# Plain FFN pairs 4 and 5: un-normalized h2 in 512 columns, weights split a chunk ahead, Strassen blocks made in between

## The chip, the cores and the metric

The kernel runs on one core of a Trainium2 chip. The metric is the device time of one execution in microseconds, as the median of several runs. Beside the runs there is one profiled execution with a trace of every instruction. Its engines are TensorE (PE; its weight loads are shown as PEld), VectorE (DVE), ScalarE (ACT), GpSimd (POOL) and the DMA queues, which are fed from SyncE (SP), ScalarE and GpSimd.

## The reference

One layer of an encoder over 512 tokens of 2048 features: a mixing part (attention over a neighbourhood and a convolution, gated, projected, normalized, added), then a feed-forward part. The change lies in the feed-forward part:

```python
u = rms_norm(h, ffn_pre_g[l])
gate, up = jnp.split(u @ w_gate_up[l], 2, axis=-1)
f = (jax.nn.silu(gate) * up) @ w_down[l]
h = h + rms_norm(f, ffn_post_g[l])
```

All is in float32. `gate` and `up` have 5632 columns each, which are 44 tiles of 128; `rms_norm` divides each token by the root of its mean square and multiplies each feature by a gain.

## The kernel before

**Layout and number format.** Features lie on the 128 partitions and the 512 tokens along the row. Each operand of a product is split into a high part, a cast to the matmul's own float32 form, and a low part, the rest. A product is then three matmuls: high weight by low activation, high by high, and low weight by high activation. ScalarE makes the high parts and VectorE the low ones (for weights `wchunk`, L137, in chunks of 128x1024; raw, high and low tiles come from pools of 5, 3 and 3). `merged` (L171) puts the high and low part of 256 tokens side by side into one tile of 512.

**The feed-forward part.** The 44 pairs of a gate tile and an up tile, counted here from 1, are made in four ways, one after the other:

- Pairs 1 and 2 (`interleaved`, L205, called at L938) read h2 times the gain, split but not yet normalized (`u`, high and low in 512 columns for each of 16 row blocks), while h2 itself is still being made.
- Pair 3 (`gemm`, L184, called at L941) reads the same `u`. In the first part of its loop, behind the first eight row blocks of the gate tile, stands the broadcast of 1/rms (`by_column`, L378) and its copy to SBUF as `r3` (L943). The pairs 1 to 3 are multiplied by `r3` when they leave PSUM (L948, L949), gated (L950, L951) and stored to DRAM from ScalarE's queue (L952). Their tiles come from a pool of two.
- Pairs 4 and 5 are the plain stage (L956 to L979). Its weights come in eight chunks of two row blocks by four tiles. For each row block, VectorE multiplies h2 by the gain and by `r3` (L964), in place; then `merged` makes two tiles of it, one for each half of the tokens; then `plain` (L178) issues three matmuls of 256 columns for each of four weight tiles and two halves. The chunk order is that of the row blocks, 0 to 15. From row block 8 on, block c and block c + 8 are joined for the Strassen part: four differences (`winograd_t`, L222) and four merges of them. At its end the gate goes through Silu straight out of PSUM (L996) and is multiplied by the up tile (L997), and `activated` (L983) stores it.
- Pairs 6 to 44 (`strassen`, L276) use a scheme with seven products of half size (Winograd's form) on the blocks `b11`, `b2`, `b_t12`, `b_t34` made in the plain stage. The first of them takes its first weight quarter from `begun` (L271).

**What sets the order.** Each engine runs its instructions in order. The order on an engine comes from the program's order and a scheduler that moves instructions by their inputs, so it is shown below as it was built. Tiles of 128x512 come from one pool of 66 slots; an instruction that writes a tile of a full pool waits until the last reader of the tile before is done.

The core of the plain stage before:

```python
for k in range(2):
    i = 2 * c + k
    nc.vector.scalar_tensor_tensor(out=f[i], in0=f[i], scalar=col(C_FPRE, i), in1=r3, op0=ALU.mult, op1=ALU.mult)
    ...
    for n in range(4):
        s = slice((k * 4 + n) * P, (k * 4 + n + 1) * P)
        for m, cols in enumerate((A, B)):
            plain(pf[n][:, cols], hi[:, s], lo[:, s], moving[m], i + m == 0, i == KT - 1)
```

Of the kernel before, what the change touches and what calls it, by code (L numbers as in the profile page):

```python
# [48 lines left out]
FT = DFF // P  # L49
# [21 lines left out]
C_PRE, C_POST, C_FPRE, C_FPOST, C_LNG, C_LNB, C_BDW, C_WDW = 0, 16, 32, 48, 64, 72, 80, 88  # L71
# [4 lines left out]
def hybrid_block(ctx: ExitStack, tc, xT, vecs, rpb, mask, w_c0, w_qk, w_v, w_gg, w_cg, w_ao, w_co, w_out, w_g0, w_gu, w_dn, outT):  # L76
    nc = tc.nc
# [6 lines left out]
    at = ctx.enter_context(tc.tile_pool(name="at", bufs=4, space=PSUM))  # L84
# [24 lines left out]
    def abank(name):  # L109
        return at.tile([P, NT], F32, tag="at", name=name)  # L110
# [60 lines left out]
    def merged(src, name):  # L171

        t = slot(name, F32R)
        nc.scalar.copy(t[:, A], src)  # L174
        nc.vector.tensor_tensor(out=t[:, B], in0=src, in1=t[:, A].bitcast(F32), op=ALU.subtract)
        return t

    def plain(o, hi, lo, t, first, last):  # L178

        nc.tensor.matmul(o, hi, t[:, B], start=first, stop=False, skip_group_check=True)  # L180
        nc.tensor.matmul(o, hi, t[:, A], start=False, stop=False, skip_group_check=True)  # L181
        nc.tensor.matmul(o, lo, t[:, A], start=False, stop=last, skip_group_check=True)  # L182

    def gemm(outs, acts, name, n=None, more=None, cols=slice(0, NT), between=(), pin=False, raw=None, load=nc.sync.dma_start):  # L184

        n = n or len(acts)
        between = iter(between)
        for c in range(0, n, 8):
            w = min(8, n - c)
            while len(acts) < c + w:  # L190
                acts.append(more(len(acts)))
            for i, (ps, src) in enumerate(outs):
                hi, lo = wchunk(src[:, c * P : (c + w) * P], f"{name}_{i}_{c}", raw=None if c or i else raw, load=load)
                for k in range(w):
                    s = slice(k * P, (k + 1) * P)
                    ah, al = (t[:, cols] for t in acts[c + k])
                    first, last = c + k == 0, c + k == n - 1
                    mmul = nc.tensor.matmul(ps, hi[:, s], al, start=first, stop=False)  # L198
# [3 lines left out]
                    nc.tensor.matmul(ps, lo[:, s], ah, start=False, stop=last)  # L202
                next(between, lambda: None)()

    def interleaved(ps, hi, lo, acts, c, cols=slice(0, NT)):  # L205
# [5 lines left out]
        for k, n, i in order:  # L211
# [10 lines left out]
    def winograd_t(u1, u2, t12, t34):  # L222

        nc.vector.tensor_tensor(out=t12[:, A], in0=u1[:, B], in1=u1[:, A], op=ALU.subtract)
        nc.vector.tensor_tensor(out=t12[:, B], in0=u2[:, B], in1=t12[:, A], op=ALU.subtract)
        nc.vector.tensor_tensor(out=t34[:, A], in0=u2[:, B], in1=u1[:, B], op=ALU.subtract)
        nc.vector.tensor_tensor(out=t34[:, B], in0=u2[:, A], in1=t12[:, B], op=ALU.subtract)
# [150 lines left out]
    def by_column(r, name, blocks=range(NB), pin=False):  # L378

        pb = abank(f"{name}_b")  # L380
        for t in blocks:
            mmul = nc.tensor.matmul(
                pb[:, t * P : (t + 1) * P], r[:, t : t + 1].broadcast_to([P, P]), ident, start=True, stop=True
            )
# [28 lines left out]
    def col(c, i):  # L413
        return vec[:, c + i : c + i + 1]
# [55 lines left out]
    u, acc = [], None  # L470
# [446 lines left out]
    for c in (*range(SPLIT), *range(HT)):  # L917
# [23 lines left out]
    gemm(  # L941
        [(pf[4 + n], w_gu[n * FT + 2]) for n in range(2)], u, "f0",
        between=(lambda: nc.scalar.copy(r3, by_column(r, "r3", pin=True)),),  # L943
    )
    for j in range(3):
        t = stp.tile([P, 2, NT], F32, tag="S", name=f"sg{j}")
        t, up = t[:, 0], t[:, 1]
        nc.vector.tensor_tensor(out=t, in0=pf[2 * j], in1=r3, op=ALU.mult)  # L948
        nc.vector.tensor_tensor(out=up, in0=pf[2 * j + 1], in1=r3, op=ALU.mult)  # L949
        nc.scalar.activation(t, t, AF.Silu)  # L950
        nc.gpsimd.tensor_tensor(out=t, in0=t, in1=up, op=ALU.mult)  # L951
        nc.scalar.dma_start(a_d[j], t)  # L952

    b11, b2, b_t12, b_t34 = [], [], [], []  # L956
    pf = [bank(f"f1_{n}") for n in range(4)]
    for c in range(HT):
        hi, lo = wchunk(w_g0[1, c], f"f1_{c}")
        if c == HT - 1:  # L960
            first = begun(w_gu[5], "f5")
        for k in range(2):
            i = 2 * c + k
            nc.vector.scalar_tensor_tensor(out=f[i], in0=f[i], scalar=col(C_FPRE, i), in1=r3, op0=ALU.mult, op1=ALU.mult)  # L964
            if i < HT:
                moving = [merged(f[i][:, cols], f"b1{i}_{n}") for n, cols in enumerate((A, B))]
                b11.append(moving[0])
            else:
                moving = [merged(f[i][:, cols], f"b2{i}_{n}") for n, cols in enumerate((A, B))]
                b2.append(moving)  # L970
            for n in range(4):
                s = slice((k * 4 + n) * P, (k * 4 + n + 1) * P)
                for m, cols in enumerate((A, B)):
                    plain(pf[n][:, cols], hi[:, s], lo[:, s], moving[m], i + m == 0, i == KT - 1)
            if i >= HT:
                t12, t34 = slot(f"t12_{i}"), slot(f"t34_{i}")
                winograd_t(f[i - HT], f[i], t12, t34)
                b_t12.append([merged(t12[:, cols], f"t12{i}_{n}") for n, cols in enumerate((A, B))])
                b_t34.append([merged(t34[:, cols], f"t34{i}_{n}") for n, cols in enumerate((A, B))])  # L979

    row = [const.tile([P, NT], F32, name=f"row{n}") for n in range(2)]

# [9 lines left out]
                nc.gpsimd.tensor_tensor(out=row[n], in0=row[n], in1=sq, op=ALU.add)  # L992

    for j in range(2):
        t = slot(f"sg{3 + j}")
        nc.scalar.activation(t, pf[2 * j], AF.Silu)  # L996
        nc.vector.tensor_tensor(out=t, in0=pf[2 * j + 1], in1=t, op=ALU.mult)  # L997
        activated(3 + j, t)


# [308 lines left out]
def _layout(x, mix_pre_g, mix_post_g, w_in, rpb, w_attn_o, w_dw, b_dw, conv_ln_g, conv_ln_b, w_conv_o, w_out,  # L1309
# [7 lines left out]
    def vec(g):  # L1317
# [13 lines left out]
    rp = rp.reshape(H, ROWS, 2, EC, ROWS, 4 * EC).transpose(0, 2, 1, 3, 4, 5)  # L1331
    wi = w_in[0]

    gu = w_gate_up[0].reshape(KT // 2, 2, P, 2, FT, P)[:, :, :, :, (0, 1, 3, 4)].reshape(KT // 2, 2, P, 2, 2, 2, P)
    gu = gu.transpose(4, 0, 2, 1, 5, 3, 6).reshape(2, KT // 2, P, 8 * P)

    cw = wi[:, 3 * CONV : 5 * CONV].reshape(KT // 2, 2, P, 2, CT, P)[:, :, :, :, :2]
    cw = cw.transpose(0, 2, 1, 4, 3, 5).reshape(KT // 2, P, 8 * P)
# [40 lines left out]
```

## Time and profile before

| what | us |
|---|---|
| median of 3 runs (2488.69 to 2489.56) | 2489.06 |
| the profiled execution | 2488.73 |
| its span, first to last instruction | 2487.0 |
| pair 3 and the broadcast, 1184.0 to 1207.9 | 23.9 |
| plain stage, 1207.9 to 1254.0 | 46.1 |
| first Strassen pair, 1254.0 to about 1273.9 | 19.9 |

Times within the span are in microseconds from its start. In a row of the timeline stand the start, the duration, the engine, the line, the operation, the tile written and the tiles read (buffer numbers left out, so that `f` is a bank of PSUM or a block of h2, `u` the split blocks, `b` and `t` the merged blocks and differences), the shape and a count. Matmuls overlap: what a matmul adds to the stream is the distance to the next start, not its own duration. The granted TensorE clock was 0.997 of full speed over the span. The engines' busy times in the three stretches:

```profile
1184.00:1207.90 23.90, 23.90 (x114) 20.02 (x114) 17.69 (x30) 10.45 (x20) 3.61 (x3) 1.00 0.37 116
1207.90:1254.00 46.10, 46.10 (x386) 46.07 (x384) 46.10 (x104) 26.64 (x62) 4.50 (x3) 1.00 0.44 130
1254.00:1274.00 20.00, 19.87 (x115) 17.35 (x114) 17.81 (x22) 11.06 (x16) 0.85 (x1) 1.00 0.71 193
```

The columns are the stretch and its length, then the busy time and count of PE, PEld, DVE, ACT and POOL, the granted clock, the share of the DMA engines and GB/s.

### The profile page before, as it was taken

To read this page: it belongs to the slowest core of one execution; us is meant where nothing else is said; L and a number is where in the kernel's file an instruction comes from. 1 tells how busy PE (TensorE), PEld (TensorE's weight loads), DVE (VectorE), ACT (ScalarE), POOL (GpSimd) and SP (SyncE) were. 2 spreads that over 40 slices of the span, in tenths; PEclk is the share of its full clock that TensorE was granted. 3 is DMA by queue.
4 is the path that set the end of the run, shared out by engine and by line. 5 is a ranking of instruction groups with operands and counts; after the bars stand their busy time and mean duration, and the time that the engine had idled before them with its cause. 6 is when DMAs were issued, how large, how long until landed. Compare 5 with 4: busy or idle time off the path is not lost. (4 is left out here: it accounts for less than half of the span.)

```text
span 2487.0 us, 36171 instructions
## 1 busy us (share of the span) xinstructions
PE 2464.5 (99%) x13495; PEld 2140.7 (86%) x13495; DVE 2073.1 (83%) x2745; ACT 1246.5 (50%) x1940; POOL 489.1 (20%) x583
## 2 busy tenths in 40 slices
PE   9999999999999999999999999999999999999997
PEld 7888888888888888888988888888888888888887
DVE  5999887497777668878898888889898889989887
ACT  5223333365555434556455555555555565456553
POOL 0110242220000000021111111122222203532352
PEclk9999999999999999999999999999999999999998
DMA  6246332486667544669466656666666778888986
GB/s 213 91 144 202 103 106 95 136 265 193 188 190 229 183 147 136 199 227 294 134 171 183 179 165 178 181 196 215 208 192 199 216 236 240 235 228 253 229 225 191
DMA packets 165249, 472.37 MB, mean 190 GB/s; under 512 B 18769, under 2 KB 30929, under 8 KB 165073
## 3 DMA queue, kind: packets, MB, share of 16 engines
q1 hardware_dynamic: 109728, 334.02, 40.3%
q0 software_dynamic: 32928, 97.54, 18.6%
q10 hardware_dynamic: 22416, 38.50, 4.1%
q8 instruction: 106, 1.74, 0.3%
q14 instruction: 71, 0.57, 0.1%
HBM read 396.06 MB, written 71.30 MB: 188 GB/s over the span
## 5 line engine op out<-in xcount | busy, mean ns | idle before, releaser
L458 DVE SCALAR_TENSOR_TENSOR cv<-z,vec,cv 128x497 f32<-128x497 f32 (+14 forms) x240 | 188.3, 786 | 4.8
L992 POOL TENSOR_TENSOR row<-row,asq 128x512 f32<-128x512 f32 x30 | 54.8, 1825 | 400.7 <-ACT asq L991 400.7
L1147 POOL TENSOR_TENSOR ys<-ys,row 128x512 f32<-128x512 f32 x32 | 57.7, 1804 | 119.7 <-DVE ys L355 99.9
L147 ACT CAST whi_qk<-raw_qk 128x1024 fp32r<-128x1024 f32 x32 | 33.7, 1054 | 79.2 <-PE qk L201 58.1
L152 DVE TENSOR_TENSOR wlo_qk<-raw_qk,whi_qk 128x1024 fp32r<-128x1024 f32 x32 | 40.4, 1262 | 37.9 <-ACT whi_qk L147 37.7
L1014 POOL TENSOR_TENSOR an<-an,row 128x512 f32<-128x512 f32 x32 | 52.1, 1630 | 74.2 <-DMA an<-a_d 49.0
L147 ACT CAST whi_y<-raw_y 128x1024 fp32r<-128x1024 f32 x31 | 32.6, 1052 | 63.0 <-PE py L201 55.2
L543 POOL TENSOR_TENSOR bm<-braw,msk 128x64 f32<-128x64 f32 x96 | 52.9, 588 | 15.5 <-DMA braw<-in_rpb 15.5
L777 DVE TENSOR_TENSOR gg<-py,gg 128x512 f32<-128x512 f32 x32 | 21.8, 687 | 39.6 <-PE py L202 33.2
L198 PE MATMUL py<-ycl,whi_y 128*128 128x512 f32 x128 | 49.8, 389 | 0.0
L201 PE MATMUL py<-ych,whi_y 128*128 128x512 f32 x128 | 49.8, 389 | 0.0
L202 PE MATMUL py<-ych,wlo_y 128*128 128x512 f32 x128 | 49.8, 389 | 0.0
L152 DVE TENSOR_TENSOR wlo_y<-raw_y,whi_y 128x1024 fp32r<-128x1024 f32 x31 | 37.8, 1224 | 14.0 <-ACT whi_y L147 8.4
L466 POOL TENSOR_TENSOR csum<-csum,cv 128x512 f32<-128x512 f32 x7 | 12.7, 1817 | 141.3 <-DVE cv L458 141.3
L181 PE MATMUL f<-b,whi_f 128*128 128x256 f32 x128 | 36.2, 283 | 0.0
L182 PE MATMUL f<-b,wlo_f 128*128 128x256 f32 x128 | 36.2, 283 | 0.0
L180 PE MATMUL f<-b,whi_f 128*128 128x256 f32 x128 | 36.2, 283 | 0.0
L147 ACT CAST whi_ca<-raw_ca 128x1024 fp32r<-128x1024 f32 x12 | 12.6, 1053 | 46.3 <-PE cb L201 18.1
L580 ACT ACTIVATE sc<-sc,st 128x256 f32<-128x256 f32 x32 | 16.1, 505 | 30.8 <-DVE st L579 30.8
L1148 POOL DMA_DIRECT2D y_d<-ys x32 | 29.4, 919 | 9.4 <-POOL ys L1147 7.8
L808 POOL DMA_DIRECT2D m_d<-m x8 | 4.4, 556 | 135.2 <-ACT m L174 95.0
L147 ACT CAST whi_v<-raw_v 128x1024 fp32r<-128x1024 f32 x16 | 16.8, 1051 | 24.2 <-PE pv L531 17.5
(3252 smaller groups left out, 8763.3 us busy)
## 6 DMA issues: line engine op xcount, KB each, us to landing
raw_qk<-in_w_qk SPq DMA_DIRECT2D x32, 512.0 KB, 3.4
raw_w<-in_w_dn SPq DMA_DIRECT2D x24, 512.0 KB, 5.6
a_d<-sg ACTq DMA_DIRECT2D x44, 256.0 KB, 4.1
raw_v<-in_w_v SPq DMA_DIRECT2D x16, 512.0 KB, 4.4
gg<-g_d SPq DMA_DIRECT2D x32, 256.0 KB, 4.0
raw_y<-in_w_co SPq DMA_DIRECT2D x16, 512.0 KB, 3.6
raw_f<-in_w_g SPq DMA_DIRECT2D x16, 512.0 KB, 3.6
an<-a_d POOLq DMA_DIRECT2D x32, 256.0 KB, 5.5
```

Of the source, the lines that this page charges most:

```text
L147: ins = cast(hi[:, s], raw[:, s])
L152: nc.vector.tensor_tensor(out=lo[:, s], in0=raw[:, s], in1=hi[:, s].bitcast(F32), op=ALU.subtract)
L180: nc.tensor.matmul(o, hi, t[:, B], start=first, stop=False, skip_group_check=True)
L181: nc.tensor.matmul(o, hi, t[:, A], start=False, stop=False, skip_group_check=True)
L198: mmul = nc.tensor.matmul(ps, hi[:, s], al, start=first, stop=False)
L201: nc.tensor.matmul(ps, hi[:, s], ah, start=False, stop=False)
L202: nc.tensor.matmul(ps, lo[:, s], ah, start=False, stop=last)
L458: nc.vector.scalar_tensor_tensor(out=a[:, to], in0=z[:, fr], scalar=col(C_WDW, i * CW + w), in1=a[:, to], op0=ALU.mult, op1=ALU.add)
L543: nc.gpsimd.tensor_tensor(out=bm[:, o + i - i0], in0=raw[:, :, min(max(i, 0), 3) * EC : (min(max(i, 0), 3) + 1) * EC], in1=msk[:, o + i - ...
L992: nc.gpsimd.tensor_tensor(out=row[n], in0=row[n], in1=sq, op=ALU.add)
L1014: ins = nc.gpsimd.dma_start(t, a_d[DN_P + k]), nc.gpsimd.tensor_tensor(out=t, in0=t, in1=row[k // KT], op=ALU.mult)
L1147: tc.keep_in_program_order(nc.gpsimd.tensor_tensor(out=t, in0=t, in1=row[n], op=ALU.mult))
```

## The change

The plain stage reads `u`, the split but un-normalized blocks that the pairs 1 to 3 read, in 512 columns, and multiplies by `r3` at the end. Its chunks hold row blocks c and c + 8, for which the weights are laid out anew on the host. In a chunk the matmuls with the high weights come first and those with the low weights behind them. The weights of chunk c + 1 are loaded and split in front of the matmuls of chunk c. The Strassen blocks of c and c + 8 are made by `prepare`, two of them within pair 3 and the others behind chunk c - 2, with the differences made in place; the second halves of the first eight blocks are not merged any more. The broadcast of 1/rms moves up in pair 3. The pairs 1 to 3 are stored from GpSimd's queue instead of ScalarE's.

```diff
-                hi, lo = wchunk(src[:, c * P : (c + w) * P], f"{name}_{i}_{c}", raw=None if c or i else raw, load=load)
                 for k in range(w):
+                    (at or {}).get((c, i, k), lambda: None)()
...
+    def prepare(c):
+
+        u1, u2 = f[c], f[c + HT]
+        for i, t in ((c, u1), (c + HT, u2)):
+            nc.vector.scalar_tensor_tensor(out=t, in0=t, scalar=col(C_FPRE, i), in1=r3, op0=ALU.mult, op1=ALU.mult)
+        b11.append(merged(u1[:, A], f"b11{c}"))
+        b2.append([merged(u2[:, cols], f"b2{c}_{n}") for n, cols in enumerate((A, B))])
+        for out, x, y in (
+            (u1[:, A], u1[:, B], u1[:, A]), (u1[:, B], u2[:, B], u1[:, B]), (u2[:, B], u2[:, B], u1[:, A]), (u2[:, A], u2[:, A], u2[:, B])
+        ):
+            nc.vector.tensor_tensor(out=out, in0=x, in1=y, op=ALU.subtract)
+        b_t12.append([merged(u1[:, A], f"t12{c}_0"), merged(u2[:, B], f"t12{c}_1")])
+        b_t34.append([merged(u1[:, B], f"t34{c}_0"), merged(u2[:, A], f"t34{c}_1")])
+
+    w = []
+
+    def next_weights():
+        w.append(wchunk(w_g0[1, len(w)], f"f1_{len(w)}"))
+
     gemm(
         [(pf[4 + n], w_gu[n * FT + 2]) for n in range(2)], u, "f0",
-        between=(lambda: nc.scalar.copy(r3, by_column(r, "r3", pin=True)),),
+        at={(0, 0, 3): lambda: nc.scalar.copy(r3, by_column(r, "r3", pin=True))},
+        between=(lambda: None, lambda: prepare(0), lambda: prepare(1), next_weights),
     )
...
-        nc.scalar.dma_start(a_d[j], t)
+        nc.gpsimd.dma_start(a_d[j], t)
...
     for c in range(HT):
-        hi, lo = wchunk(w_g0[1, c], f"f1_{c}")
-        if c == HT - 1:
+        if c + 1 < HT:
+            next_weights()
+        else:
             first = begun(w_gu[5], "f5")
-        for k in range(2):
...
+        hi, lo = w[c]
+        acts = list(enumerate((u[c], u[c + HT])))
+        for part in range(2):
+            for k, (ah, al) in acts:
+                for n, ps in enumerate(pf):
+                    s = slice((k * 4 + n) * P, (k * 4 + n + 1) * P)
+                    if part:
+                        nc.tensor.matmul(ps, lo[:, s], ah, start=False, stop=c + k == HT, skip_group_check=True)
+                    else:
+                        nc.tensor.matmul(ps, hi[:, s], al, start=c + k == 0, stop=False, skip_group_check=True)
+                        nc.tensor.matmul(ps, hi[:, s], ah, start=False, stop=False, skip_group_check=True)
+        if c + 2 < HT:
+            prepare(c + 2)
...
-        t = slot(f"sg{3 + j}")
-        nc.scalar.activation(t, pf[2 * j], AF.Silu)
-        nc.vector.tensor_tensor(out=t, in0=pf[2 * j + 1], in1=t, op=ALU.mult)
+        t, up = slot(f"sg{3 + j}"), slot(f"su{3 + j}")
+        nc.vector.tensor_tensor(out=t, in0=pf[2 * j], in1=r3, op=ALU.mult)
+        nc.vector.tensor_tensor(out=up, in0=pf[2 * j + 1], in1=r3, op=ALU.mult)
+        nc.scalar.activation(t, t, AF.Silu)
+        nc.vector.tensor_tensor(out=t, in0=t, in1=up, op=ALU.mult)
```

Three places as the engines now have them. Names are those of the program with their buffer numbers; what an instruction waits for stands in brackets, by the engine or DMA queue that gives the signal.

TensorE at the plain stage, before: `f1_0` to `f1_3` are the four banks, `b10_0` and `b10_1` the merged halves of row block 0.

```order
L180 MATMUL f1_2_10966<-b10_0_10975,whi_f1_0_10969 128x256
L181 MATMUL f1_2_10966<-b10_0_10975,whi_f1_0_10969 128x256
L182 MATMUL f1_2_10966<-b10_0_10975,wlo_f1_0_10970 128x256
L180 MATMUL f1_2_10966<-b10_1_10978,whi_f1_0_10969 128x256
L181 MATMUL f1_2_10966<-b10_1_10978,whi_f1_0_10969 128x256
L182 MATMUL f1_2_10966<-b10_1_10978,wlo_f1_0_10970 128x256
```

And in the change, where the high weights of chunk 0 end and its low ones follow (`u2_8l` and `u2_8h` are row block 8 of `u`):

```order
L980 MATMUL f1_2_11026<-u2_8l_10614,whi_f1_0_11001 128x512
L981 MATMUL f1_2_11026<-u2_8h_10613,whi_f1_0_11001 128x512
L980 MATMUL f1_3_11027<-u2_8l_10614,whi_f1_0_11001 128x512
L981 MATMUL f1_3_11027<-u2_8h_10613,whi_f1_0_11001 128x512
L978 MATMUL f1_0_11024<-u2_0h_10351,wlo_f1_0_11002 128x512
L978 MATMUL f1_1_11025<-u2_0h_10351,wlo_f1_0_11002 128x512
```

Six matmuls of 256 columns on one bank became three of 512, and the third of them moved behind the chunk's sixteen with high weights.

VectorE in the change, from the second pass of the first gated tile (`sg0`) to the third tile (`sg2`), whose buffer is that of `sg0`:

```order
L959 TENSOR_TENSOR sg0_11006<-f0_1_10348,r3_10806 128x512
L958 TENSOR_TENSOR sg1_11012<-f0_2_10349,r3_10806 128x512
L959 TENSOR_TENSOR sg1_11012<-f0_3_10350,r3_10806 128x512
L152 TENSOR_TENSOR wlo_f1_1_11030<-raw_f1_1_11028,whi_f1_1_11029 128x1024 [waits DMAHW5_49,PE_49,Activation_49]
L935 SCALAR_TENSOR_TENSOR f2_10008<-f2_10008,vec_75,r3_10806 128x512
L935 SCALAR_TENSOR_TENSOR f10_10040<-f10_10040,vec_75,r3_10806 128x512 [waits DMAHW4_49]
L958 TENSOR_TENSOR sg2_11018<-f0_4_10818,r3_10806 128x512 [waits DMASW6_49,Pool_49]
```

Before, the row of `sg2` (L948) waited for a store from ScalarE's queue and stood eighteen rows behind the second pass of `sg0`; it now waits for one from GpSimd's (DMASW) and stands six rows behind.

VectorE at the start of pair 6, before (`f5l` are low weights, `f5s` and `f6s` weight sums, `f_1` and `f_3` banks, `f5v` copies out of PSUM):

```order
L266 TENSOR_TENSOR f5l<-f5s_11771,f5h 128x1024 [waits Activation_49]
L355 TENSOR_TENSOR sg_11845<-f_3_11703,f5c_11799 128x256 [waits Activation_49]
L288 TENSOR_TENSOR f6s_11891<-f6s_11857,f6q 128x1024 [waits DMAHW5_49,DMASW7_49,DVE_49]
L329 TENSOR_TENSOR f_1_11679<-f_1_11679,f5v_11726 128x512 [waits PE_49]
L266 TENSOR_TENSOR f5l<-f5s_11724,f5h 128x1024 [waits Activation_49]
```

And in the change:

```order
L254 TENSOR_TENSOR f5l<-f5s_11545,f5h 128x1024 [waits Activation_49]
L317 TENSOR_TENSOR f_1_11453<-f_1_11453,f5v_11500 128x512 [waits PE_49]
L254 TENSOR_TENSOR f5l<-f5s_11498,f5h 128x1024 [waits DVE_49,Activation_49]
L343 TENSOR_TENSOR sg_11619<-f_3_11477,f5c_11573 128x256 [waits DVE_49]
L276 TENSOR_TENSOR f6s_11665<-f6s_11631,f6q 128x1024 [waits DMAHW2_49,DMASW2_49,DVE_49]
```

The sum into the bank (L329, now L317) stood behind the weight sum of pair 7 (L288, now L276) and now stands three rows ahead of it.

More of the change, by code (lines that the diff above doesn't have):

```diff
@@ L176, in merged, with gemm @@
         return t
[L178 to L184, printed above, removed]
+    def gemm(outs, acts, name, n=None, more=None, cols=slice(0, NT), between=(), pin=False, raw=None, load=nc.sync.dma_start, at=None):
         n = n or len(acts)
@@ L220, in interleaved @@
                 follow(nc.tensor, mmul)
[L222 to L227, printed above, removed]
     def winograd_in_place(u):
@@ L940, in hybrid_block @@
     pf += [abank(f"f0_{n}") for n in range(4, 6)]
+    b11, b2, b_t12, b_t34 = [], [], [], []
+    def prepare(c):
[13 more added lines that the diff above has]
+        w.append(wchunk(w_g0[1, len(w)], f"f1_{len(w)}"))
     gemm(
         [(pf[4 + n], w_gu[n * FT + 2]) for n in range(2)], u, "f0",
-        between=(lambda: nc.scalar.copy(r3, by_column(r, "r3", pin=True)),),
+        at={(0, 0, 3): lambda: nc.scalar.copy(r3, by_column(r, "r3", pin=True))},
+        between=(lambda: None, lambda: prepare(0), lambda: prepare(1), next_weights),
     )
@@ L951, in hybrid_block @@
         nc.gpsimd.tensor_tensor(out=t, in0=t, in1=up, op=ALU.mult)
-        nc.scalar.dma_start(a_d[j], t)
-    b11, b2, b_t12, b_t34 = [], [], [], []
+        nc.gpsimd.dma_start(a_d[j], t)
     pf = [bank(f"f1_{n}") for n in range(4)]
     for c in range(HT):
-        hi, lo = wchunk(w_g0[1, c], f"f1_{c}")
-        if c == HT - 1:
+        if c + 1 < HT:
+            next_weights()
+        else:
             first = begun(w_gu[5], "f5")
-        for k in range(2):
[L963 to L979, printed above, removed]
+        hi, lo = w[c]
[11 more added lines that the diff above has]
+            prepare(c + 2)
     row = [const.tile([P, NT], F32, name=f"row{n}") for n in range(2)]
@@ L1332, in _layout @@
     wi = w_in[0]
-    gu = w_gate_up[0].reshape(KT // 2, 2, P, 2, FT, P)[:, :, :, :, (0, 1, 3, 4)].reshape(KT // 2, 2, P, 2, 2, 2, P)
-    gu = gu.transpose(4, 0, 2, 1, 5, 3, 6).reshape(2, KT // 2, P, 8 * P)
+    gu = w_gate_up[0].reshape(KT, P, 2, FT, P)
+    gu = [
+        gu[:, :, :, n : n + 2].reshape(*by, P, 2, 2, P).transpose(*order, 2, 1 - order[0], 4, 3, 5).reshape(KT // 2, P, 8 * P)
+        for n, by, order in ((0, (KT // 2, 2), (0,)), (3, (2, KT // 2), (1,)))
+    ]
     cw = wi[:, 3 * CONV : 5 * CONV].reshape(KT // 2, 2, P, 2, CT, P)[:, :, :, :, :2]
@@ L1354, in _layout @@
         w_out=tiles(w_out[0]),
-        w_g0=c(gu),
+        w_g0=np.stack(gu),
         w_gu=tiles(w_gate_up[0]),
```

## Prediction, made before the changed kernel ran

> **What bounds the kernel now.** I read the busy shares first, then what TensorE waited for, then the stage that the change touches by windows, then its rows one by one.
>
> ```profile
> PE 2464.5 (99%) x13495; PEld 2140.7 (86%) x13495; DVE 2073.1 (83%) x2745; ACT 1246.5 (50%) x1940; POOL 489.1 (20%) x583
> PE warm L123 <- POOL ident masks.py:199: 1.5, 1, 1.5
> ...
> PE r_s L365 <- ACT ysq L1223: 0.2, 1, 0.2
> 1207.93:1253.99 46.06, 46.06 (x385) 46.06 (x384) 46.06 (x104) 26.63 (x62) 4.50 (x3) 1.00 0.44 130
> ```
>
> The first row is the page's: TensorE is busy for 99% of the span. The next two are the first and the last of the twelve rows of what its matmuls waited for; the twelve add up to 8.2 us in 2487. The last is the windows' row of the plain stage of pairs 4 and 5 (columns: PE, PEld, DVE, ACT and POOL busy, granted clock, DMA share, GB/s). TensorE and VectorE are both busy for all of it and the granted clock is 1.00. So time can go here only where TensorE's own stream gets shorter; and VectorE, with no gap of its own, is the engine to watch for a new wait.
>
> A full row of digits does not say at what rate matmuls follow each other. That is in the starts:
>
> ```profile
> 1197.05 0.39 PE L198 MATMUL f<-u_8l,whi_f 128*128 128x512 f32 x1
> ...
> 1207.70 0.39 PE L202 MATMUL f<-u_15h,wlo_f 128*128 128x512 f32 x1
> 1207.93 0.28 PE L180 MATMUL f<-b,whi_f 128*128 128x256 f32 x1
> 1208.04 0.28 PE L181 MATMUL f<-b,whi_f 128*128 128x256 f32 x1
> ...
> 1253.88 0.28 PE L182 MATMUL f<-b,wlo_f 128*128 128x256 f32 x1
> 1254.00 0.40 PE L304 MATMUL f<-b,f5h 128*128 128x512 f32 x1
> ```
>
> From 1197.05 to 1207.93 stand the last 48 matmuls of pair 3, each over 512 columns: 10.88 / 48 = 0.2267 us from start to start. From 1207.93 to 1254.00 stand the 384 matmuls of the plain stage, each over 256 columns: 46.07 / 384 = 0.1200 us. Two of 256 columns take 0.2400, one of 512 takes 0.2267. Twice the columns cost 0.1067 more, so about 0.0133 us of each matmul has nothing to do with its columns (0.1200 - 0.1067).
>
> **The change part by part. TensorE's stream.** The 384 matmuls of 256 columns become 192 of 512, over the same columns in all. At pair 3's spacing, same operand forms and same tiles of h2, they take 192 x 0.2267 = 43.52 us in place of 46.07: **2.55 us less**, all of it on the path, as TensorE waits for nothing in the stage.
>
> The Trainium skill speaks against the size of this: "TensorE: Matmul & The Clock Gate", section Back-to-back issue gap, gives an isolated gap of N / 2.4 + 2.5 ns at full clock, which is 109.2 ns for 256 columns and 215.8 for 512. By that estimate the saving would be 192 x (218.4 - 215.8) = 0.5 us. The rows above differ from it (120.0 and 226.7 ns), and they decide.
>
> **Row of 1/rms sooner.** The broadcast of 1/rms goes from behind the first eight row blocks of the pair 3 GEMM to in front of the fourth, that is 15 matmuls or 3.4 us up.
>
> ```profile
> 1185.52 1.03 POOL L375 TENSOR_TENSOR r_r<-r_v,mhalf 128x4 f32<-128x4 f32 x1 [8.93 <-DVE r_v L373]
> 1187.28 0.39 PE L198 MATMUL f<-u_3l,whi_f 128*128 128x512 f32 x1
> 1190.68 1.05 PE L382 MATMUL r_b<-ident,r_r 128*128 128x128 f32 x8
> 1191.77 0.59 ACT L943 COPY r<-r_b 128x512 f32<-128x512 f32 x1
> 1132.38 1.63 POOL L375 TENSOR_TENSOR r_r<-r_v,mhalf 128x2 f32<-128x2 f32 x1 [12.13 <-DVE r_v L373]
> ```
>
> The power on GpSimd ends at 1186.55; TensorE now gets to the broadcast at 1187.28, where the row of the fourth block starts. That leaves 0.7 us. The same step took 1.63 at 1132.38, and would then end at 1187.15, still before. So no wait; the bound on the other side is 0.5 us, if the notice takes longer than I allow. The broadcast costs TensorE the same at either place. The row in SBUF is there at 1191.77 + 0.59 - 3.4 = 1188.96, and VectorE may begin 3 us sooner.
>
> **VectorE's and ScalarE's work.** The old code split both halves of all 16 blocks (32 merges); the new one leaves out the second half of the first eight, which nothing else reads: 8 merges less on each engine. The differences and their merges stay. The end of the stage gets four VectorE passes more (both pairs must now be multiplied by 1/rms), 4 x 0.60.
>
> ```profile
> 1192.87 0.68 DVE L948 TENSOR_TENSOR sg<-f,r 128x512 f32<-128x512 f32 x1
> 1193.47 0.68 DVE L949 TENSOR_TENSOR sg<-f,r 128x512 f32<-128x512 f32 x1
> 1230.30 0.41 DVE L224 TENSOR_TENSOR t<-f 128x256 f32<-128x256 f32 x1
> 1230.64 0.41 DVE L226 TENSOR_TENSOR t<-f,f 128x256 f32<-128x256 f32 x1
> 1237.48 1.40 DVE L964 SCALAR_TENSOR_TENSOR f<-f,vec,r 128x512 f32<-128x512 f32 x2
> 1238.80 0.74 DVE L175 TENSOR_TENSOR b<-f,b 128x256 fp32r<-128x256 f32 x2
> 1246.30 1.21 DVE L266 TENSOR_TENSOR f5l<-f5q,f5h 128x1024 fp32r<-128x1024 f32 x1
> 1247.44 1.08 DVE L175 TENSOR_TENSOR t<-t,t 128x256 fp32r<-128x256 f32 x3
> ```
>
> Start to start: 0.60 for a pass over 512 columns of PSUM, 0.34 for 256 columns, 0.66 for a scaling pass (1.32 for two), 1.14 for a weight's low part. From 1188.96 VectorE then has 16 scalings, 56 merges, 32 differences, 9 low parts and 6 passes over PSUM: 10.6 + 19.0 + 10.9 + 10.3 + 3.6 = 54.4 us, done at 1243.4 if nothing holds it. TensorE leaves the stage at 1207.93 + 43.52 = 1251.45. So there are 8 us to spare where there was no gap. Slots could eat some: h2 stays held for the stage, and later blocks wait until TensorE has used up a chunk. The last block may start when the sixth of eight chunks is done, at 1240.6, and needs about 5 us. That still ends by 1247. Cost: **nothing**. The sooner blocks buy nothing either, since TensorE did not wait for them.
>
> **The store that goes to another queue.** The three stores of gated tiles go from ScalarE's queue to GpSimd's. Their tiles come from a pool of two, so the first write of the third tile stands behind the first store, on VectorE, and its Silu stands on ScalarE ahead of the cast of the third weight chunk.
>
> ```profile
> 1194.30 1.29 POOL L951 TENSOR_TENSOR sg<-sg 128x512 f32<-128x512 f32 x1 [7.75 <-ACT sg L950]
> 1210.31 2.73 POOL L951 TENSOR_TENSOR sg<-sg 128x512 f32<-128x512 f32 x1 [12.32 <-ACT whi_f L147]
> 1223.90 0.91 POOL L253 DMA_DIRECT2D f5s<-in_w_gu  x1 [10.86 <-DMA f5s<-in_w_gu]
> y_d<-yf POOLq DMA_DIRECT2D x16, 256.0 KB, 3.9
> y_d<-y_d POOLq DMA_DIRECT2D x8, 512.0 KB, 9.2
> ```
>
> VectorE has 30 instructions up to the second half of the first tile (4 scalings, 22 of 256 columns, 2 low parts, 2 passes: 2.6 + 7.5 + 2.3 + 1.2 = 13.6 us), so the tile is whole at 1202.6. The product takes 1.3 to 2.7 us, the store 3.9 (the nearest, a plain store of this size) to 9.2 (the slowest of GpSimd's queue shown): free at 1207.8 to 1214.5. VectorE gets there at 1202.6 + 3.7 = 1206.3, and stands still for 1.5 to 8.2 us. The third chunk's cast then follows by 0.60 + 0.6 (Silu) + 1.05, at 1210.1 to 1216.8; A chunk is 24 matmuls, 5.44 us, and TensorE wants the third at 1207.93 + 2 x 5.44 = 1218.8. Hidden by 2 to 9 us; I take the near end. If that cover goes, each us later is a us of the total.
>
> The Trainium skill has a rule against this move: "SBUF — State Buffer", section SBUF: two separate sides, warns that a DMA issued by GpSimd can starve, as its descriptors need a port that VectorE may hold. By it the store could cost much more than 9.2 us. The row at 1223.90 has GpSimd issue one in 0.91 us while VectorE was busy without a gap, which speaks against that here.
>
> **The next pair.** In pair 6, the first of the Strassen part, TensorE waited once:
>
> ```profile
> 1262.97 1.21 DVE L288 TENSOR_TENSOR f6s<-f6s,f6q 128x1024 f32<-128x1024 f32 x1
> 1264.10 0.69 DVE L329 TENSOR_TENSOR f<-f,f5v 128x512 f32<-128x512 f32 x1
> 1264.82 0.59 ACT L293 COPY f5v<-f 128x512 f32<-128x512 f32 x1 [1.88 <-DVE f L329]
> 1265.46 1.01 PEld L304 LDWEIGHTS f<-t,f5l 128*128 128x128 f32 x8 [0.33 <-ACT f5v L293]
> ```
>
> The sum at 1264.10 stood behind a weight sum for pair 7 that took 1.13; in the new order it stands ahead of that. Walked from 1251.0, when the first bank of the stage is complete: five passes (3.0), a low part, a pass, a low part, a weight sum, a pass, a low part (4 x 1.14 + 2 x 0.60) bring VectorE to 1259.8; the product that the sum needs ends about 1260.1; the sum and the copy are done by 1261.5. TensorE wants them at about 1265.13 - 2.55 = 1262.6. So the 0.33 us go as well. Bounds: 0.33 gained, or up to 1 us lost if one cast comes late, as the margin is 1.1 us. I take the gain. Behind it, from pair 8 on, the engines' orders are the old ones.
>
> **Sum.** -2.55 - 0.33 = -2.88 us. The profiled execution took 2488.73 (span 2487.0 and 1.7 around it), 0.33 under the median of the three runs, 2489.06. Its span would be 2484.1, and the median **2486.2**.
>
> **The rivals.** *Columns are all that costs.* If what a matmul takes beside its columns doesn't halve with their number, 192 matmuls of 512 columns come out 0.2400 apart, and only the 0.33 us of pair 6 go: **2488.7**. Against it stand the 48 matmuls of pair 3; for it, a little, that the same shape ran slower for a stretch:
>
> ```profile
> 1151.59 0.40 PE L215 MATMUL f<-u_4h,whi_f 128*128 128x512 f32 x1
> ...
> 1152.98 0.84 PE L215 MATMUL f<-u_4l,whi_f 128*128 128x512 f32 x3
> ```
>
> These are six in 1.39 us, 0.232 each, which would leave 1.6 of the 2.55 us. This rival is also what the rule of the Trainium skill above comes close to.
>
> *The gain is taken back in pair 6.* The four new passes and two Silus stand in front of its weight casts, and the one wait of 0.33 us there becomes one of 1 to 2.5 us: **2487.5** to 2489. For: the margin is 1.1 us. Against: the walk above, with the weight sum out of the way.
>
> *Slower.* The store on GpSimd's queue holds VectorE and, by the Silu, the third weight cast. It decides from a store of 9.2 + 2.0 = 11.2 us on; from 14.1 the kernel is slower than before, as 2.9 us of gain are used up, and at 20 us it stands at 2486.2 + 8.8 = **2495**. For: VectorE is dense there, and a GpSimd product took 2.73 instead of 1.29 in that place. Against: the issue row and landings of 3.9.
>
> *More than the sum.* VectorE's spare 8 us let later stages run without waits. The twelve rows total 8.2 us, most of them far away (warm-up, the last norm), so more than 5 us in all would need nearly all of them to go: **2483**.
>
> That the change does not do what it says I leave out: the order shows 192 matmuls of 512 columns.
>
> **How the numbers follow.** A measurement of this kernel can tell about 0.2% from no change, which is 5.0 us here; the forecast of 0.12% lies inside. Forecast 0.72, columns alone 0.06, pair 6 takes it back 0.10, slower rival 0.08 (over half of it past 0.2%), more than the sum 0.04. Faster by over 0.2%: 0.05; within: 0.90; slower: 0.05. The forecast's bounds are 0.5 for the broadcast, 1.3 for pair 6 and some 0.4 between runs: 2485.0 to 2488. With the two rivals that give the gain back, the range goes from 2484.8 to 2489.0, and leaves out the slower rival, the faster one and a little more.
>
> **What would show it.** In the new profile: 192 matmuls from the first chunk to pair 6 in 43.5 us, 0.2267 apart; no wait at the broadcast in front of the fourth block; the third gated tile's first pass some us late on VectorE with no gap on TensorE behind it; no wait before pair 6's third sum with its copy. Wrong would be a gap on TensorE at the third or fourth chunk (the store), a spacing over 0.23, or a longer gap in pair 6.

## The result, and the profile after

The changed kernel takes **2484.77 us** (median of 19 runs, 2484.23 to 2487.94) against 2488.80 of the kernel before in the same runs (19, 2487.86 to 2492.44): ratio 0.9986 [0.9979, 0.9992], 4.0 us less. That is inside the 0.2% that was called no change, though the interval leaves out 1. It was forecast at 2486.2; the median lies 1.4 us under that and rounds to the low end of the range, 2484.8. So the size of the gain is what has to be explained: 2.9 us were forecast, and 4.0 came.

Where it came from can't be read off the span alone. The profiled executions took 2485.70 (span 2483.9) and 2488.73 (span 2487.0), but from one execution to another the part ahead of the plain stage and the part behind pair 7 differ by 1 us or more, while the stage and the pairs behind it repeat to some 0.02 us. So the stretches are compared one by one.

Of the kernel after: the page's row of busy time, then the windows' rows of the plain stage and of pair 6, in the columns used above, then TensorE's rows at the two ends of the stage.

```profile
PE 2462.1 (99%) x13303; PEld 2131.3 (86%) x13303; DVE 2073.4 (83%) x2741; ACT 1245.3 (50%) x1932; POOL 492.9 (20%) x586
```

```profile
1208.08:1251.60 43.52, 43.52 (x194) 36.04 (x193) 42.49 (x89) 23.51 (x51) 6.81 (x4) 1.00 0.52 143
1251.60:1271.10 19.50, 19.50 (x113) 17.20 (x112) 18.29 (x23) 11.42 (x16) 0.84 (x1) 1.00 0.71 215
```

```profile
1207.85 0.39 PE L197 MATMUL f<-u_15h,wlo_f 128*128 128x512 f32 x1
1208.08 0.39 PE L980 MATMUL f<-u_0l,whi_f 128*128 128x512 f32 x1
...
1251.60 1.98 PE L292 MATMUL f<-b,f5h 128*128 128x512 f32 x8
```

The stage takes 43.52 us where it took 46.07, and pair 6 takes 19.50 where it took 19.91 (1254.00 to 1273.91). That is 2.55 + 0.41 = 2.96 us. From pair 7 to pair 44, TensorE's starts lie 2.81 us earlier throughout, to 0.01 us (0.15 of the 2.96 was lost ahead of the stage, in that one execution). What is left of the 4.0 us has to lie elsewhere, and it was found at the very end. Here are the last row of VectorE (timeline, with the answer's heading that gives the span) and the issues of the last stores (name, queue, count, size, median us from issue to landing), first of the kernel before, then of the kernel after.

```profile
core 0 of [0], span 2487.0 us
2480.57 1.29 DVE L1287 TENSOR_TENSOR yg<-yg,hb 128x512 f32<-128x512 f32 x2
```

```profile
out<-yg ACTq DMA_DIRECT2D x3, 256.0 KB, 4.9
out<-hb POOLq DMA_DIRECT2D x1, 512.0 KB, 7.1
```

```profile
core 0 of [0], span 2483.9 us
2478.53 1.29 DVE L1293 TENSOR_TENSOR yg<-yg,hb 128x512 f32<-128x512 f32 x2
```

```profile
out<-yg ACTq DMA_DIRECT2D x3, 256.0 KB, 4.2
out<-hb POOLq DMA_DIRECT2D x1, 512.0 KB, 6.2
```

The last VectorE result is there at 2481.86 before and at 2479.82 after; the span ends 5.14 us later before, and 4.08 us later after. The last stores, which no line of the diff touches, land about 1 us sooner. Nothing in the prediction speaks of this; the section on the store below shows what moved.

### The profile page after: what moved, and what is told of

It is laid out like the page before. It is cut to its first block, busy times and chain, and to the rows that moved or that the text cites. A ratio compares the mean times of both kernels' runs of the same rounds, so it can differ in the third digit from the quotient of the medians.

```text
span 2483.9 us, 35789 instructions
## 1 busy us (share of the span) xinstructions
PE 2462.1 (99%) x13303; PEld 2131.3 (86%) x13303; DVE 2073.4 (83%) x2741; ACT 1245.3 (50%) x1932; POOL 492.9 (20%) x586
## 5 line engine op out<-in xcount | busy, mean ns | idle before, releaser
L1083 DVE TENSOR_TENSOR sg<-sg,su 128x512 f32<-128x512 f32 x39 | 28.9, 740 | 0.0
L193 PEld LDWEIGHTS py<-ycl,whi_y 128*128 128x128 f32 x128 | 24.0, 188 | 5.0
L197 PEld LDWEIGHTS py<-ych,wlo_y 128*128 128x128 f32 x128 | 24.0, 188 | 5.0
```

The costliest lines, as they stand in the source:

```text
L1083: nc.vector.tensor_tensor(out=t, in0=t, in1=up, op=ALU.mult)
```

## Experiments

Each kernel's stretches, from the starts on TensorE and the last VectorE result ("end"), in us, and its median less that of the kernel before in the same runs. "Sum" adds up the differences of stage, pair 6 and end against the kernel before.

| kernel | stage | pair 6 | end | sum | median difference |
|---|---|---|---|---|---|
| before | 46.07 | 19.91 | 5.14 | 0 | 0 |
| after | 43.52 | 19.50 | 4.08 | -4.02 | -4.03 |
| after, again | 43.52 | 19.51 | 3.84 | -4.25 | -3.76 |
| halves | 46.08 | 19.53 | 4.03 | -1.48 | -1.74 |
| no weights ahead | 43.52 | 19.51 | 3.83 | -4.26 | -3.23 |
| late row | 43.52 | 19.90 | 3.72 | -3.98 | -3.79 |
| sum held in program order, in before | 46.07 | 19.90 | 5.47 | +0.32 | +0.37 |
| sum ahead, in before | 46.07 | 19.53 | 5.12 | -0.40 | -0.37 |
| two merges again | 43.52 | 23.87 | 3.77 | +0.04 | +1.16 |
| four merges again | 43.95 | 28.15 | 3.78 | +4.76 | +5.26 |
| store from ScalarE | 43.52 | 19.50 | 5.39 | -2.71 | -2.49 |
| store from ScalarE, again | 43.52 | 19.50 | 5.18 | -2.92 | -2.65 |

The three stretches account for each median to within 1.1 us, about the spread between executions; that they meet it to 0.01 us for the kernel after is chance. Two merges also takes 0.30 us more in pair 7 (19.81 in place of 19.51), which its sum leaves out.

### The stage: is it the number of matmuls?

**Halves** is the kernel after with each matmul of 512 columns cut into two of 256; all else of the change stays.

```diff
-    nc.tensor.matmul(ps, lo[:, s], ah, ...)
+    for q in range(0, NT, 256):
+        cs = slice(q, q + 256)
+        nc.tensor.matmul(ps[:, cs], lo[:, s], ah[:, cs], ...)
```

> The changed kernel, with each matmul of the plain stage issued as two over 256 columns each, in the new order and with everything else as it is: 384 matmuls again. Theory (about 0.0133 us of each matmul has nothing to do with its columns, so the gain of the stage is a matter of the count): the stage takes 46.1 us instead of 43.5, the kernel 2.55 us more than the changed one, and stays some 0.4 to 0.5 us under the one before. Rival (the gain came with the earlier row of 1/rms, the earlier weights or the lighter VectorE): the stage stays at 43.5 to 44 us and the kernel within 0.5 us of the changed one.

The stage goes back to 46.08 us, pair 6 stays at 19.53, and the kernel takes 2487.22 (ratio 0.9992 [0.9983, 1.0001]). The first row of the stage and the first of pair 6, from TensorE's timeline:

```profile
1208.78 0.28 PE L982 MATMUL f<-u_0l,whi_f 128*128 128x256 f32 x1
...
1254.86 1.32 PE L292 MATMUL f<-b,f5h 128*128 128x512 f32 x5
```

So the 2.55 us are the count of matmuls and nothing else of the change. **Quarters** cuts them into four of 128 columns in the same way.

> The changed kernel with each matmul of the plain stage issued as four over 128 columns: 768 matmuls. Theory (0.0133 us beside the columns for each, and 0.1067 us for 256 columns): 0.0667 us from start to start, 51.2 us for the stage, the kernel 7.7 us over the changed one. Rival (below some width the weight load sets the pace, which the records show at 0.19 us each but overlapped): the spacing stays near 0.10 to 0.12 us, the stage takes 77 to 92 us, and the kernel is 33 to 48 us slower.

In the one run of it the stage takes 85.71 us and the kernel 2527.59: 768 matmuls at 0.1116 us. My theory (0.0667) fell; a matmul of 128 columns is hardly shorter than one of 256. **Widths** cuts the columns in another way in each chunk.

```diff
+WIDTHS = cut(512), cut(256, 256), cut(384, 128), cut(128, 128, 128, 128), cut(320, 192), cut(*[64] * 8), cut(448, 64), cut(512)
...
+    for q0, q1 in WIDTHS[c]:
+        cs = slice(q0, q1)
```

> The kernel after, with the 512 columns of the plain stage cut in another way in each of its eight chunks of weights: 512; 256+256; 384+128; 128 four times; 320+192; 64 eight times; 448+64; 512. The same products are added up. My theory, a fixed 0.0133 us and 0.1067 us per 256 columns from 256 columns on: spacing 0.2267 us at 512, 0.200 at 448, 0.173 at 384, 0.147 at 320, 0.120 at 256. Below 256 columns two theories: a floor (nothing is quicker than the 0.1116 us of the kernel in quarters: 192, 128 and 64 columns all 0.11, and the chunk of 64 columns takes 192 x 0.11 = 21 us), or four passes instead of one for narrow matmuls (the columns count, but at twice the price or more: 0.06 to 0.07 at 64, 0.16 to 0.18 at 192, and the chunk of 64 columns takes 12 to 13 us).

It ran once. The windows of its first chunks, cut at the starts on TensorE, and of what followed (columns as above; the granted clock is the third number from the end):

```profile
1207.10:1212.54 5.44, 5.44 (x25) 4.51 (x24) 5.44 (x14) 3.53 (x9) 3.17 (x1) 1.00 0.33 98
1212.54:1218.29 5.75, 5.75 (x49) 5.75 (x48) 5.75 (x10) 2.38 (x6) 1.88 (x2) 1.00 0.41 152
1218.29:1225.12 6.83, 6.83 (x51) 6.83 (x49) 6.83 (x17) 3.15 (x8) 0.90 (x1) 1.00 0.56 152
1225.12:1235.84 10.72, 10.72 (x98) 10.72 (x97) 9.86 (x20) 5.26 (x11) 0.00 (x0) 1.00 0.43 128
1235.84:1242.06 6.22, 6.22 (x51) 6.22 (x50) 4.31 (x9) 1.83 (x5) 0.00 (x0) 1.00 0.47 171
1242.06:1247.90 5.84, 5.84 (x55) 5.84 (x54) 4.65 (x10) 2.78 (x6) 0.86 (x1) 1.00 0.62 121
1247.90:1291.60 43.70, 43.70 (x189) 42.66 (x189) 5.48 (x12) 4.01 (x7) 0.00 (x0) 0.50 0.11 33
```

A chunk is 24 products of 512 columns. 512: 5.44 / 24 = 0.2267 us. 256 + 256: 5.75 / 48 = 0.1198. 128 four times: 10.72 / 96 = 0.1117. 384 + 128: 6.83 / 24 = 0.285, which is 0.1733 + 0.1117. 320 + 192: 6.22 / 24 = 0.259, which is 0.1467 + 0.1117 to 0.001. So from 256 columns on, the law of the prediction holds (0.0133 us and 0.1067 us per 256 columns), and below 256 there is a floor of 0.1117 us. The rows for 64 columns start 0.111 us apart too, up to 1247.80, so the theory of four passes (0.06 to 0.07 us there) is out. PEld is busy for the whole of every chunk that holds a cut of 256 columns or fewer, and for 4.51 of 5.44 us in the chunk of 512, so the weight load ahead of each matmul is what I take the floor for; that is argued, not shown. At 1247.90 the granted clock fell to 0.50, so the rest of this run, the cut into 448 columns too, can't be read against the law.

The Trainium skill ("TensorE: Matmul & The Clock Gate", section Back-to-back issue gap) gave isolated gaps of 109.2 and 215.8 ns for 256 and 512 columns; by the estimate from them only 0.5 us were to be had. The stages of the two kernels measure 120.0 and 226.7 ns, and the 2.55 us were there: the measurement decides.

**No weights ahead** takes two more edits out: the weights are split in their own chunk again (those of the first chunk stay in pair 3), and each low-weight matmul follows its high ones.

```diff
-        if c + 1 < HT:
+        if c:
             next_weights()
...
-        for part in range(2):
-            for k, (ah, al) in acts:
...
+        for k, (ah, al) in acts:
```

> The changed kernel with the weights of a chunk loaded and split in the chunk itself, and the matmuls with low weights back behind their high ones instead of at the chunk's end. Theory (TensorE never waits for weights in the stage, since the scheduler and the buffers run ahead anyway): within 0.3 us of the changed kernel. Rival (these two edits are what keeps TensorE fed while VectorE makes blocks): a wait of 0.5 to 2 us at the low weights of several chunks, 3 to 8 us in all.

Stage and pair 6 are those of the kernel after, and the time can't be told from its time (2485.30; ratio to before 0.9989 [0.9980, 0.9998]). These two edits neither gain nor cost.

### Pair 6: why did TensorE wait there, and why does it not now?

The prediction blamed the order on VectorE: the sum behind the weight sum of pair 7. The first attempt to test that in the kernel before held the sum at its place in the program's order.

```diff
-        nc.vector.tensor_tensor(out=y, in0=y, in1=p1, op=ALU.add)
+        add = nc.vector.tensor_tensor(out=y, in0=y, in1=p1, op=ALU.add)
+        if name == "f5":
+            tc.keep_in_program_order(add)
```

> The kernel before, with one instruction kept in program order: the sum into the bank in pair 6 that stood behind the weight sum of pair 7. Theory: TensorE's wait of 0.33 us there goes, the distance from the first matmul of pair 6 to that of pair 7 goes from 19.9 to 19.5 us, and the kernel is 0.4 us under the one before, which the runs will hardly tell. Rival (the wait is set by the cast or the copy on ScalarE): the wait stays.

It missed its aim: the weight sum (L288) still stood ahead of the sum, the wait of 0.33 us stayed, and pair 6 took 19.90 us (ratio 1.0001 [0.9993, 1.0010]). It says nothing on the cause. **Late row** is the kernel after with the broadcast of 1/rms back behind the first eight row blocks:

```diff
-        at={(0, 0, 3): lambda: nc.scalar.copy(r3, by_column(r, "r3", pin=True))},
-        between=(lambda: None, lambda: prepare(0), ...),
+        between=(lambda: nc.scalar.copy(r3, by_column(r, "r3", pin=True)), lambda: prepare(0), ...),
```

> The changed kernel with the broadcast of 1/rms back behind the first eight row blocks. VectorE starts its blocks 3.4 us later. As the prediction had it (8 us to spare on VectorE): no change in time, within 0.3 us of the changed kernel. Rival, from the changed kernel's trace, where VectorE has no gap from 1189.1 to 1250.1 and then only 1.0 us idle: VectorE reaches the end of the stage some 2.4 us late, the scheduler puts other work there too, and TensorE waits 1 to 2.5 us in pair 6.

Timeline of the late row in pair 6 (which starts at 1251.05):

```profile
1261.12 0.68 DVE L317 TENSOR_TENSOR f<-f,f5v 128x512 f32<-128x512 f32 x1
1261.83 0.59 ACT L281 COPY f5v<-f 128x512 f32<-128x512 f32 x1 [0.41 <-DVE f L317]
1262.47 1.01 PEld L292 LDWEIGHTS f<-t,f5l 128*128 128x128 f32 x8 [0.32 <-ACT f5v L281]
1263.19 1.20 DVE L276 TENSOR_TENSOR f6s<-f6s,f6q 128x1024 f32<-128x1024 f32 x1
```

Here the weight sum stands behind the sum, as in the kernel after, and the wait is back all the same: VectorE comes to the sum 10.07 us after the pair's start. In the kernel after (pair 6 from 1251.60) it comes at 8.55:

```profile
1260.15 0.70 DVE L317 TENSOR_TENSOR f<-f,f5v 128x512 f32<-128x512 f32 x1 [0.20 <-PE f L292]
1260.88 0.59 ACT L281 COPY f5v<-f 128x512 f32<-128x512 f32 x1 [0.58 <-DVE f L317]
1261.79 2.08 PE L292 MATMUL f<-t,f5l 128*128 128x256 f32 x16
```

**Sum ahead** is the kernel before with only the order of those two turned round.

```diff
+            if name == "f6" and i == 2:
+                issued_behind(ins, adds[-1])
...
+        adds.append(add)
```

> The kernel before, with one instruction moved on VectorE: the first weight sum of pair 7 now stands behind the fifth merge sum of pair 6, as in the kernel after, and nothing else is changed. My theory (the prediction's step on pair 6): TensorE waits 0.33 us in pair 6 because that sum stands behind the weight sum of 1.21 us, so here the wait goes and pair 6 takes 19.5 us instead of 19.91, with the stage still at 46.07 and the time some 0.4 us under the kernel before, which the medians cannot tell from none. Rival (from the kernel with the late row): VectorE reaches pair 6 too late because the row comes late, and the order on it does not matter; then pair 6 stays at 19.9 and the wait of 0.3 us stays.

Its timeline in pair 6, which starts at 1253.99:

```profile
1262.96 0.69 DVE L333 TENSOR_TENSOR f<-f,f5v 128x512 f32<-128x512 f32 x1
1263.67 0.59 ACT L297 COPY f5v<-f 128x512 f32<-128x512 f32 x1 [0.74 <-DVE f L333]
1264.21 2.08 PE L308 MATMUL f<-t,f5l 128*128 128x256 f32 x16
1264.69 1.21 DVE L290 TENSOR_TENSOR f6s<-f6s,f6q 128x1024 f32<-128x1024 f32 x1
```

The sum starts 8.97 us after the pair's start (in the kernel before 10.10), the wait is gone, and pair 6 takes 19.53 us. The median, 0.37 us under before (ratio 0.9998 [0.9989, 1.0007]), cannot tell that from none; the trace can. So what counts is when the sum starts: with 10.1 us the wait comes, with 9.0 it doesn't. In the kernel before the order alone made it late. In the changed kernel the earlier row is needed as well.

### VectorE's spare time

**Two** and **four merges again** repeat low halves of merges on VectorE, two or four for each pair of row blocks, with the values unchanged: 5.4 and 10.8 us more of its work.

```diff
+        for _ in range(1):
+            for t, src in zip(b_t34[-1], (u1[:, B], u2[:, A])):
+                nc.vector.tensor_tensor(out=t[:, B], in0=src, in1=t[:, A].bitcast(F32), op=ALU.subtract)
```

> The changed kernel with two merges of each pair of blocks repeated on VectorE (the same result again): 16 passes of 0.34 us, 5.4 us more on VectorE within the stage. As the prediction had it (8 us to spare): no change in time. Rival (VectorE's spare time in the changed kernel is about 1 us, and 1.3 us more in pair 6): TensorE waits about 3 us in pair 6, and the kernel is about 3 us over the changed one.

> The same with 32 passes, 10.8 us more on VectorE. As the prediction had it (8 us to spare): 2 to 3 us over the changed kernel. Rival (about 2.3 us to spare): 8 to 9 us over it, the waits at the start of pair 6, with the weight casts of chunks 6 and 7 still in time.

Two: stage 43.52, pair 6 23.87, kernel 2489.69 (ratio 1.0002 [0.9993, 1.0011]). Four: 43.95 and 28.15, kernel 2493.79 (1.0022 [1.0013, 1.0031]). Of the 5.4 us, 4.37 come out in pair 6 and 0.30 in pair 7; of the 10.8 us, 8.65 come out in pair 6 and 0.43 in the stage. So 0.7 and 1.7 us of them were hidden, not 8. The longest single wait, in the timeline of the two:

```profile
1263.13 0.69 DVE L317 TENSOR_TENSOR f<-f,f5v 128x512 f32<-128x512 f32 x1
1265.06 1.11 PEld L292 LDWEIGHTS f<-t,f5l 128*128 128x128 f32 x8 [2.60 <-ACT f5v L281]
```

It is the same matmul as in the late row, now held 2.60 us (TensorE's own row names a weight's low part, L254, as what it waited for, so the sum alone may not be to blame); the rest of the 4.37 us is spread over other waits in pair 6. One reservation: the scheduler also put weight sums of pair 6 behind the passes at the end of the stage, so part of the 4.37 us may be due to the order.

### The store on the other queue

**Store from ScalarE** is the kernel after with that one line as in before; on every other engine, and in the rest of these two, the order of instructions is the same.

```diff
-        nc.gpsimd.dma_start(a_d[j], t)
+        nc.scalar.dma_start(a_d[j], t)
```

> The changed kernel with the three stores of pairs 1 to 3 back on ScalarE's queue. Theory (the store was hidden): within 0.3 us of the changed kernel, no new wait on TensorE. Rival (the move to GpSimd's queue was worth something, as it takes waits for the gating product off ScalarE): ScalarE stands still for 1 to 3 us more at the three stores, and the kernel is 0.5 to 1.5 us slower than the changed one.

It took 2486.47 (ratio 0.9992 [0.9983, 1.0001]), with the stage and pair 6 as in the kernel after, so the cause of the extra time was not in the place where I looked. Both kernels were run again, on one chip:

> The kernel after, word for word, beside the next one on the same chip. Theory: stage 43.52 us, pair 6 19.50, and a median 3 to 4.5 us under the kernel before.

> The kernel after with the store of the four row blocks' weight sums issued by ScalarE instead of GpSimd, again. My theory: the store is hidden on either queue, so the stage takes 43.52 us, pair 6 19.50, and the median is within 0.3 us of the kernel after in the same rounds. Rival: the first run's median of 1.7 us more was the queue's doing; then it is again 1 us or more above, and the trace has to show where.

The edit of the last one is the one line shown above, the three stores of gated tiles; the store of weight sums that its text names was not touched.

After: 2485.25 (11 runs, 2483.13 to 2487.04; ratio 0.9982 [0.9973, 0.9991]). With the store from ScalarE: 2486.36 (11 runs, 2485.64 to 2490.10; 0.9990 [0.9981, 0.9999]). It is 1.1 us more again, as the rival had it, though the two intervals overlap. The end of this kernel, from the same views as for the other two above:

```profile
core 0 of [0], span 2484.6 us
2478.13 1.29 DVE L1293 TENSOR_TENSOR yg<-yg,hb 128x512 f32<-128x512 f32 x2
```

```profile
out<-yg ACTq DMA_DIRECT2D x3, 256.0 KB, 5.0
out<-hb POOLq DMA_DIRECT2D x1, 512.0 KB, 7.1
```

From the last VectorE result to the span's end it is 5.18 us (5.39 in the first run). In all 14 traces, those with the three stores on ScalarE's queue have 5.12 to 5.47 us there (five traces, of four kernels: the store from ScalarE twice, and before with its two variants), and those with them on GpSimd's have 3.72 to 4.08 (nine). The two groups don't touch. So the queue of three stores near 1210 us decides how soon the last stores land, 1270 us later.

How it does stands a few rows further up in the same timelines. `hb` is the tile of the 512 KB store that GpSimd issues at the end. First the kernel after, then the store from ScalarE, again:

```profile
2471.24 1.21 DVE L1287 TENSOR_TENSOR hb<-yg,r_b 128x1024 f32<-128x1024 f32 x1
2472.75 1.37 POOL L1289 DMA_DIRECT2D out<-hb  x1 [0.85 <-DVE hb L1287]
```

```profile
2470.84 1.21 DVE L1287 TENSOR_TENSOR hb<-yg,r_b 128x1024 f32<-128x1024 f32 x1
2473.56 1.37 POOL L1289 DMA_DIRECT2D out<-hb  x1 [2.06 <-DVE yg L1287]
```

In the kernel after GpSimd issues this store 0.30 us after VectorE has written `hb`. With the three early stores on ScalarE's queue the trace has it released by the next VectorE row (`yg`), and it is issued 1.51 us after `hb`. All 14 traces divide in this way: 0.29 to 0.31 us in the nine, 1.50 to 1.51 in the five. So the big store starts 1.2 us later against VectorE's rows. It is then still under way when VectorE is done (2473.56 + 7.1 = 2480.7 against 2479.42), where in the kernel after it had landed (2472.75 + 6.2 = 2479.0 against 2479.82), and the stores of `yg` on ScalarE's queue take 5.0 us in place of 4.2. That the late store is what delays them fits all 14 traces, but no run moved that store alone. Why the program as built makes it wait for one row more was not found; the order of instructions on VectorE and GpSimd is the same there.

## Why the prediction was right, and where it was not

**The stage: right.** 192 x 0.2267 = 43.52 us, and 43.52 came; halves shows that the count of matmuls alone makes the difference. The rival in which only columns cost is out.

**The broadcast without a wait: right in the kernel after, with a margin that doesn't always do.** The timeline of the kernel after:

```profile
1185.66 1.03 POOL L363 TENSOR_TENSOR r_r<-r_v,mhalf 128x4 f32<-128x4 f32 x1 [9.29 <-DVE r_v L361]
1187.42 1.05 PE L370 MATMUL r_b<-ident,r_r 128*128 128x128 f32 x8
1188.51 0.59 ACT L952 COPY r<-r_b 128x512 f32<-128x512 f32 x1 [2.83 <-PE r_b L370]
1189.13 1.41 DVE L935 SCALAR_TENSOR_TENSOR f<-f,vec,r 128x512 f32<-128x512 f32 x2 [2.20 <-ACT r L952]
```

The row lands at 1189.10, 0.14 later than forecast. In the second run of the store from ScalarE, the same power took twice as long, and TensorE waited:

```profile
1185.52 2.08 POOL L363 TENSOR_TENSOR r_r<-r_v,mhalf 128x4 f32<-128x4 f32 x1 [9.23 <-DVE r_v L361]
1187.65 1.16 PE L370 MATMUL r_b<-ident,r_r 128*128 128x128 f32 x8 [0.26 <-POOL r_r L363]
```

From the sum of squares to the stage that execution took 24.21 us where the others took 23.64: a price of 0.57 us, a little over the bound of 0.5. In the other 13 traces the power took 1.03.

**"There are 8 us to spare", "the sooner blocks buy nothing": wrong.** VectorE's end of the stage in the kernel after:

```profile
1248.87 1.22 DVE L254 TENSOR_TENSOR f5l<-f5q,f5h 128x1024 fp32r<-128x1024 f32 x1
1251.11 0.69 DVE L1000 TENSOR_TENSOR sg<-f,r 128x512 f32<-128x512 f32 x1 [1.03 <-PE f L978]
```

It worked without a gap up to 1250.1, not 1243.4. Its own groups of instructions say why: beside the 54.4 us counted, it did four rows of pair 6 in the stage (two weight sums and two low parts, 4 x 1.14 = 4.6 us), and two of the 16 scalings, each beside a GpSimd product, took 1.83 and 1.78 us instead of 0.74, 2.1 us more together (below): 61.1, and 61.0 are there. I counted the stage's work and let the free time lie idle, though work of pair 6 stood ready to fill it. The free time was real, but it belonged to pair 6, where the sum's start has about 1 us to spare (10.1 us after the pair's start is too late, 9.0 is in time). The late row shows what the sooner blocks buy: 0.4 us.

**The store: hidden where I looked, mis-sized, and not free.** In the kernel after it landed within 2.3 to 2.9 us, against the 3.9 to 9.2 allowed, and VectorE did not stand still. Timeline there:

```profile
1204.47 0.64 POOL L962 DMA_DIRECT2D a_d<-sg  x1 [0.31 <-POOL sg L961]
1205.13 1.30 POOL L961 TENSOR_TENSOR sg<-sg 128x512 f32<-128x512 f32 x1
1205.17 2.49 DVE L935 SCALAR_TENSOR_TENSOR f<-f,vec,r 128x512 f32<-128x512 f32 x2
1207.58 0.68 DVE L958 TENSOR_TENSOR sg<-f,r 128x512 f32<-128x512 f32 x1
```

The third tile's first pass (1207.58) follows the scalings at once. The slower rival is out. What the Trainium skill ("SBUF — State Buffer", section SBUF: two separate sides) warns of, that a DMA issued by GpSimd may starve, did not show here: the issue took 0.64 us beside a VectorE without a gap. But the store's queue was worth 1.1 to 1.6 us at the kernel's end (4.08 and 3.84 us against 5.39 and 5.18), most likely by the longer wait of the `hb` store. That is the term that the sum lacked: -2.55 - 0.41 - 1.06 = -4.02, and the median moved by -4.03. The prediction had no reason for a gain there, and the range held it only because its low end happened to lie 1.4 us under the forecast; that part of being right is luck.

**Pair 6: the gain right, its cause half.** The wait of 0.33 us went, with 0.41 us of time. The walk gave the product's end as 1260.1 and the copy as done at 1261.5, and the trace has 1260.15 and 1261.47. But the order that the prediction named is the cause only in the kernel before (sum ahead); in the changed one the row's time is as much needed. The rival "taken back in pair 6" did not come, but it was near: a late row or 5.4 us more on VectorE bring it, as the late row and the two merges show. The fourth rival, "more than the sum", was right in its sign, with another cause than the one named.

## What to carry to other kernels

Where TensorE never waits, read the distance between starts for each width of matmul and count matmuls: a wide one saves the fixed part, and here a matmul of fewer than 256 columns was hardly cheaper than one of 256 (0.1117 us against 0.1200). Before you call an engine's free time spare, follow its order to the next stage that waits for it, as the scheduler fills the time with that stage's work. And when a sum of local terms doesn't meet the measured time, compare the traces from both ends, and read what each DMA issue waited for: here moving three stores changed the wait of another store 1270 us later.

## What was unexpected of the hardware

- One store of 512 KB issued 1.2 us later went with slower landings of it (7.1 to 7.4 us against 5.8 to 6.2 on GpSimd's queue) and of the three last stores on ScalarE's queue (4.9 to 5.3 us against 3.9 to 4.2). Five traces stand against nine; that the transfers slow each other is argued, not shown.
- In widths, TensorE's clock fell from 1.00 to 0.50 at 1247.9 us, 5.8 us into matmuls of 64 columns, with no wait on TensorE, and stayed there to about 1291.6; the spacing went from 0.111 to 0.213 us. In quarters, 85.7 us of matmuls of 128 columns kept the full clock. The Trainium skill ("TensorE: Matmul & The Clock Gate", Part 1: The HAM clock gate) has the clock set to half or full by how busy the array has been; that it can fall without a gap between matmuls is what this one run adds.
- A VectorE scaling with two inputs from SBUF that started 0.04 us behind a GpSimd product of 1.30 us took 1.83 us instead of 0.74 (the row at 1205.17 puts it together with the next one). A second one, at 1213.60, took 1.78 us beside a GpSimd product that itself took 4.49 us where the other two took 1.30.
